# Moving three VectorE sums one step later in the queue of a blocked matrix product

## The chip, the cores and the metric

The kernel runs on one core of one Trainium2 chip. The metric is the time of one execution on the device, in microseconds (us). The profile is taken by the hardware profiler on one further execution; its span runs from the first to the last instruction.

## The reference

One layer of a diffusion transformer with a mixed sequence mixer, batch 1, 512 tokens, width 2048, float32. What matters here is the feed-forward part at its end:

```python
def conv_ffn(h, w_up, conv_w, conv_b, w_down):
    u, g = jnp.split(h @ w_up, 2, -1)
    return (u * jax.nn.silu(dwconv3(g, conv_w, conv_b))) @ w_down
...
    hx = modulate(x, sh2, sc2)
    fx = from_rows(conv_ffn(to_rows(hx), w_up[l], ffn_conv_w[l], ffn_conv_b[l], w_down[l]))
    x = layer_norm(ALPHA * x + g2 * fx, ln2_g[l], ln2_b[l])
```

`h` is 512 x 2048, `w_up` is 2048 x 11264 (u and g halves of 5632 columns each), `w_down` 5632 x 2048. `dwconv3` is a convolution of three taps along rows of 64 tokens. Ahead of it come the modulation vectors, the input projection, a gated linear recurrence in both directions, a pooling and a short convolution, and the output projection.

## The kernel before

Products of float32 are made from three products of halves: each matrix is split into a high part (a cast, on ScalarE) and a low part (what the cast left, a subtraction on VectorE). `mm3` (L109 to L113) issues high x high (L111), high x low (L112) and low x high (L113) into one PSUM place.

The changed lines belong to the stage `up_pair`, which runs 20 times, for pairs p = 2 to 21 of 128-column blocks of `w_up`, about 1330 to 2176 us into the span. Each call makes two blocks with `up_block`: first the gate's (tiles with `_g`), then u's (`_u`). A block is the product of 512 tokens with 256 columns over a depth of 2048, and is computed by a scheme of seven products over a 2 x 2 partition, as Strassen's: sums of weights and sums of activations go into seven smaller products, and four sums on VectorE give the result (L1026 to L1029, the evictions). The activations' sums (S1 to S4) are made before the stage.

A block goes through its depth in two steps (`8 // NB`, NB = 4). For each step `weights7` prepares the weights:

- the tile W, in three slots (two in the pool `ww`, one in `w3`, taken by the counter `wcount`), is loaded by two transfers of 512 KB, issued by SyncE (L989);
- three sums on VectorE fill its remaining places (L992 with 128 x 1024 elements, L993 and L994 with 128 x 512 each, each reading what the one before wrote);
- `parts` is called twice (NU = 2 of the four depth blocks each): a cast to H on ScalarE (L973), 128 x 1792 elements, and the subtraction to L on VectorE (L974). H and L have three buffers each. In what follows these are the first and the second low part of a step.

Each half step is then 7 x 2 x 3 = 42 matmuls of 128 x 256, a step 84, a pair of blocks 336. A slot of W is free again when the step's second low part is made; a buffer of H or L when TensorE has read it.

Between the blocks VectorE also makes two instructions of the gate's convolution (L936, L938) and a product with the sigmoid (L1042) for each of two column blocks, and after u's block the last products (L1047), which POOL's queue stores to `h_d`.

The order on each engine's queue is fixed when the program is traced, by a scheduler that takes what is ready in its own estimate of time, by priority; `high_priority(offset=AHEAD)` lets the weights' work go 600 places ahead of its place in the text. An engine then carries out its queue in that order, and waits where an instruction's inputs are not there. What `issue_after(x)` adds is a demand on this order alone: an instruction traced inside stands behind x in their engine's queue; it adds no signal between engines.

The stage after it, `down`, uses `parts` too, for `w_down`.

Of the kernel before, what the change touches and what calls it, by code (L numbers as in the profile page):

```python
# [1 line left out]

# [1 line left out]

# [5 lines left out]
F32 = mybir.dt.float32  # L10
# [3 lines left out]
ALU = mybir.AluOpType  # L14
# [8 lines left out]
H = 8  # L23
# [49 lines left out]
class Kernel:  # L73
# [436 lines left out]
    def pair(self, xp, gp, p, Tx, Vx):  # L510
        nc = self.nc
        qs, Qs, gs = [], [], []
        b = self.proj_x(f"q{p}", 256 * p)
        for h in range(2):
            sg = gp.tile([P, L], F32, name=f"sq_{p}_{h}", tag="sig", bufs=1)
            nc.scalar.activation(out=sg, in_=b[h], func=AF.Sigmoid)
            q = gp.tile([P, L], F32, name=f"q_{p}_{h}", tag="o", bufs=16)
            nc.vector.tensor_tensor(out=q, in0=b[h], in1=sg, op=ALU.mult)
            qs.append(q)
        if p < 2:  # L520
            T, V = Tx[p], Vx[p]
        else:
            V = xp.tile([P, NTT, 256], F32, name=f"v_{p}", tag="v", bufs=2)
            b = self.proj_x(f"v{p}", DH + 256 * p, natural=True)
            for i in range(2):
                nc.scalar.copy(out=V[:, 2 * i:2 * i + 2].rearrange("p a b -> p (a b)"), in_=b[i])
        b = self.proj_x(f"g{p}", 4 * DH + 256 * p)
        for h in range(2):
            g = gp.tile([P, L], F32, name=f"g_{p}_{h}", tag="o", bufs=16)
            nc.scalar.activation(out=g, in_=b[h], func=AF.Sigmoid)  # L530
            nc.vector.tensor_tensor(out=g, in0=b[h], in1=g, op=ALU.mult)
            gs.append(g)
        if p >= 2:
            T = [xp.tile([P, 2, L], F32, name=f"T_{2 * p + h}", tag="t", bufs=4) for h in range(2)]
        K = [xp.tile([P, 2, L], F32, name=f"K_{2 * p + h}", tag="k", bufs=2) for h in range(2)]
        for d in range(2):
            zs = [t[:, 1 - d] for t in T]
            if p >= 2:
                zs = self.proj_x(f"f{d}{p}", DH * (2 + d) + 256 * p)
            for h in range(2):  # L540
                self.gates(zs[h], T[h], K[h], d, d * H + 2 * p + h)
        for h in range(2):
            Q = gp.tile([P, 2, L], F32, name=f"Q_{p}_{h}", tag="Q", bufs=2)
            nc.vector.tensor_tensor(out=Q, in0=vw(qs[h][:, :], [[0, 2], [1, L]]), in1=T[h], op=ALU.mult)
            Qs.append(Q)
        self.steps = [self.gla(gp, 2 * p + h, qs[h], Qs[h], K[h], T[h], V[:, :, h * P:(h + 1) * P], gs[h])
                      for h in range(2)]
        self.bg_calls = 0
# [419 lines left out]
    def parts(self, ww, name, src, n):  # L968

        nc = self.nc  # L970
        H = ww.tile([P, 7 * NU * P], F32R, name=f"H_{name}", tag="H", bufs=3)
        Lw = ww.tile([P, 7 * NU * P], F32R, name=f"L_{name}", tag="L", bufs=3)
        nc.scalar.copy(out=H[:, 0:n], in_=src)  # L973
        nc.vector.tensor_tensor(out=Lw[:, 0:n], in0=src, in1=H[:, 0:n].bitcast(F32), op=ALU.subtract)  # L974
        return H, Lw

    def weights7(self, ww, name, src, c0):

        nc = self.nc
        tt = nc.vector.tensor_tensor
        with self.tc.high_priority(offset=AHEAD):
            pool, n = (ww, 2) if self.wcount % 3 < 2 else (self.w3, 1)
            self.wcount += 1
            W = pool.tile([P, NB, 7, P], F32, name=f"W_{name}", tag="W", bufs=n)
            for r0, s0 in ((c0, 2), (c0 + KT // 2, 0)):
                nc.sync.dma_start(out=vw(W[:, 0, 0, :], [[7 * P, NB], [1, 2 * P]], s0 * P),  # L989
                                  in_=src[r0 * P:(r0 + NB) * P].rearrange("(k p) c -> p k c", p=P))  # L990
            pair = lambda a, b: vw(W[:, 0, 0, :], [[7 * P, NB], [(b - a) * P, 2], [1, P]], a * P)
            tt(out=pair(4, 3), in0=pair(3, 1), in1=pair(2, 3), op=ALU.subtract)  # L992
            tt(out=W[:, :, 5], in0=W[:, :, 1], in1=W[:, :, 4], op=ALU.subtract)  # L993
            tt(out=W[:, :, 6], in0=W[:, :, 0], in1=W[:, :, 5], op=ALU.subtract)  # L994
            units = []
            for c in range(0, NB, NU):
                units += self.parts(ww, f"{name}_{c}", W[:, c:c + NU].rearrange("p a s m -> p (a s m)"), 7 * NU * P),
        return units

    def up_block(self, ww, ep, name, src):  # L1000
# [177 lines left out]
    def run(self):  # L1178
        tc, nc = self.tc, self.nc
        self.setup()  # L1180
        self.mods2 = self.persist.tile([P, 4 * KT], F32, name="mods2")
        self.o = [None] * KT
        self.h_d = [self.dram.tile([P, L], F32, name=f"h_d{f}") for f in range(NFF)]
        self.y_d = [self.dram.tile([P, 4, 512], F32, name=f"y_d{t}") for t in range(NTT)]
        self.g2_d = self.dram.tile([1, D], F32, name="g2_d")
        self.y, self.h2, self.S, self.h = {}, ({}, {}), {}, {}
        self.upc = self.wcount = 0
        with tc.tile_pool(name="wts", bufs=1, reuse_waits="tile", side="right") as self.wts:
            with tc.tile_pool(name="xp", bufs=1, reuse_waits="tile") as xp:
                self.xp = xp  # L1190
                with tc.tile_pool(name="rp", bufs=1, reuse_waits="tile") as rp:
                    self.setup_columns1(rp)
                    self.load_in(xp, rp)
                    self.setup_columns2(rp)
                    Tx, Vx = self.ramp(xp, rp)
                with tc.tile_pool(name="gp", bufs=1, reuse_waits="tile") as gp:
                    self.bg, self.bg_due, self.steps, self.bg_calls = self.ada_rest(gp), 0.0, [], 0
                    for p in (0, 2, 3):
                        self.pair(xp, gp, p, Tx, Vx)
                    self.local_setup(gp)  # L1200
                    self.conv(gp, 0)
                    self.pair(xp, gp, 1, Tx, Vx)
                    self.pool(gp, 0)
                    self.pool(gp, 1)
                    self.conv(gp, 1)
                    for st in (self.bg, *self.steps):
                        for _ in st:
                            pass
                    self.split_o()
            hctx = ExitStack()  # L1210
            hx = hctx.enter_context(tc.tile_pool(name="hx", bufs=1, reuse_waits="tile"))
            with tc.tile_pool(name="hq", bufs=1, reuse_waits="tile") as hq:
                with tc.tile_pool(name="cp", bufs=1, reuse_waits="tile") as cp:
                    st0 = self.out_half(cp, 0)
                    self.norm_mid(cp, hx, hq, 0, st0)
                    st1 = self.out_half(cp, 1)
                    for p in range(SPLIT_PAIRS):
                        self.up_half(cp, p, 0)
                    raw = self.norm_mid(cp, hx, hq, 1, st1)
                    nc.sync.dma_start(out=self.g2_d.rearrange("o (k p) -> (o p) k", p=P), in_=self.mods2[:, 3 * KT:4 * KT])  # L1220
                    for p in range(SPLIT_PAIRS):
                        self.up_half(cp, p, 1)
                        self.combine(cp, raw, (2 * p, 2 * p + 1))
        gap = self.ctx.enter_context(tc.tile_pool(name="gap", bufs=1, side="right", reuse_waits="tile"))
        gap.tile([P, 112], F32, name="gap_right")
        with tc.tile_pool(name="ww", bufs=1, reuse_waits="tile", side="right") as ww:
            with tc.tile_pool(name="ep", bufs=1, reuse_waits="tile") as ep, \
                    tc.tile_pool(name="w3", bufs=1, side="right", reuse_waits="tile") as self.w3:
                for p in range(SPLIT_PAIRS, NFF // 2):
                    self.up_pair(ww, ep, p)  # L1230
            hctx.close()
            with tc.tile_pool(name="dn", bufs=1, reuse_waits="tile") as dn:
                f0 = 0
                for i, n in enumerate(PORTIONS[:-1]):
                    self.down(ww, dn, f0, n, i == 0)
                    f0 += n
                self.finish(ww, dn, f0, PORTIONS[-1])
# [28 lines left out]
```

## Time and profile before

| | |
|---|---|
| time, median of 3 runs | 2684.64 us (2683.98 to 2686.53) |
| the profiled execution | 2687.12 us |
| its span | 2685.3 us |
| mean granted TensorE clock | 0.985 |
| TensorE busy (matmul) | 2545.6 us, 95% |
| VectorE busy | 1897.1 us, 71% |
| ScalarE busy | 928.8 us, 35% |
| GpSimd busy | 256.1 us, 10% |

Engines in the profile: PE is TensorE, PEld its weight loads, DVE VectorE, ACT ScalarE, POOL GpSimd, SP SyncE; a name with a q at its end is that engine's sequencer, which issues transfers and waits. A line of the view of waits names who waited, the source line, what ended the wait, then microseconds in total, times, and the longest. A line of a timeline gives start and length in microseconds, engine, source line, operation, tile written and tiles read, shapes, a count where several were merged, and in brackets the idle time just before it and what ended it. The granted clock is the share of full speed at which the profile says that TensorE was clocked.

### The profile page before, as it was taken

How to read it: one execution, taken by the hardware profiler on the slowest of the kernel's cores; microseconds unless marked ns; L12 is line 12 of the kernel's file. 1: busy time of each engine (PE TensorE's matmuls, PEld its weight loads, DVE VectorE, ACT ScalarE, POOL GpSimd, SP SyncE). 2: the span in 40 equal slices, each digit the busy share in tenths (PEclk: the TensorE clock that was granted, in tenths of full speed). 3: DMA queues.
4: the chain of work that ended last, by engine and by line, in shares of the span. 5: the costliest groups of instructions: out<-in, count | busy, mean ns of one | idle time of the engine just before them, and what ended most of it. 6: DMA issues, size and time to landing. Idle time of an engine off the chain costs nothing.

```text
span 2685.3 us, 40002 instructions
## 1 busy us (share of the span) xinstructions
PE 2545.6 (95%) x16332; PEld 2240.9 (83%) x16332; DVE 1897.1 (71%) x2408; ACT 928.8 (35%) x1119; POOL 256.1 (10%) x255
## 2 busy tenths in 40 slices
PE   5999999999999999999899999999999899999996
PEld 4677998888878888769899999999999888888885
DVE  5543569968698866778988889888898864433338
ACT  5221254232333324354543334433343342222111
POOL 0120102213051300001100000000000000000005
PEclk9999999999999999999999999999999999999998
DMA  8755236756646546657533333333333374333321
GB/s 266 235 181 164 87 95 224 235 167 197 204 148 209 160 128 207 209 188 243 160 111 120 109 110 118 111 107 117 116 104 125 103 247 155 127 122 131 109 94 63
DMA packets 301461, 409.85 MB, mean 153 GB/s; under 512 B 17669, under 2 KB 193117, under 8 KB 300765
## 3 DMA queue, kind: packets, MB, share of 16 engines
q1 hardware_dynamic: 297692, 395.76, 45.8%
q0 software_dynamic: 3584, 11.54, 1.1%
q8 instruction: 128, 2.10, 0.4%
q14 instruction: 57, 0.46, 0.1%
HBM read 387.30 MB, written 19.93 MB: 152 GB/s over the span
## 4 chain that ended last, share of the span: by engine, by line
PE 55%; DVE 19%; DMA 15%; issue 6%; ACT 2%; POOL 1%; SPq 1%; DVEq 0%; POOLq 0%; ACTq 0%
DMA W_g<-in_w_up_dram 7%; DMA W_u<-in_w_up_dram 6%; PE dn L113 6%; PE dn L112 6%; PE dn L111 5%; DVE L_g L974 3%; DVE L_u L974 3%; DVE W_u L992 2%; PE wo L112 2%; PE wo L113 2%; PE wo L111 1%; PE rx L111 1%; PE rc L111 1%; PE rx L113 1%; PE rc L112 1%
## 5 line engine op out<-in xcount | busy, mean ns | idle before, releaser
L974 DVE TENSOR_TENSOR L_dn<-W_dn,H_dn 128x1536 fp32r<-128x1536 f32 (+1 forms) x56 | 96.2, 1719 | 223.2 <-ACT H_dn L973 223.2
L973 ACT CAST H_u<-W_u 128x1792 fp32r<-128x1792 f32 x80 | 135.6, 1695 | 174.1 <-PE ub_g L112 171.9
L682 DVE SCALAR_TENSOR_TENSOR aacc<-a,csil,aacc 128x512 f32<-128x512 f32 x240 | 188.7, 787 | 8.3 <-DMA a<-in_w_ada_dram 3.2
L113 PE MATMUL dn<-H_dn,hl 128*128 128x512 f32 x480 | 188.6, 394 | 0.0
L112 PE MATMUL dn<-L_dn,hh 128*128 128x512 f32 x480 | 188.2, 392 | 0.0
L111 PE MATMUL dn<-H_dn,hh 128*128 128x512 f32 x480 | 185.9, 388 | 0.0
L973 ACT CAST H_dn<-W_dn 128x1536 fp32r<-128x1536 f32 (+1 forms) x56 | 81.4, 1453 | 294.9 <-PE dn L113 290.3
L974 DVE TENSOR_TENSOR L_u<-W_u,H_u 128x1792 fp32r<-128x1792 f32 x80 | 161.5, 2018 | 2.5 <-ACT H_u L973 2.5
L974 DVE TENSOR_TENSOR L_g<-W_g,H_g 128x1792 fp32r<-128x1792 f32 x80 | 161.4, 2018 | 1.0 <-ACT H_g L973 1.0
L973 ACT CAST H_g<-W_g 128x1792 fp32r<-128x1792 f32 x80 | 135.0, 1689 | 75.8 <-PE ub_g L112 55.7
L113 PE MATMUL ub_g<-h2h,L_g 128*128 128x256 f32 x480 | 137.8, 288 | 23.8 <-DVE L_g L974 23.3
L113 PE MATMUL ub_u<-h2h,L_u 128*128 128x256 f32 x480 | 136.3, 284 | 22.4 <-DVE L_u L974 22.4
L111 PE MATMUL ub_g<-h2h,H_g 128*128 128x256 f32 x480 | 134.6, 280 | 8.5 <-ACT H_g L973 8.5
L112 PE MATMUL ub_g<-h2l,H_g 128*128 128x256 f32 x480 | 134.4, 280 | 0.0
L112 PE MATMUL ub_u<-h2l,H_u 128*128 128x256 f32 x480 | 132.9, 277 | 0.0
L111 PE MATMUL ub_u<-h2h,H_u 128*128 128x256 f32 x480 | 132.8, 277 | 0.0
L105 ACT CAST wh_r<-wr_r 128x1024 fp32r<-128x1024 f32 x48 | 50.3, 1048 | 208.1 <-PE rc L113 112.4
L113 PEld LDWEIGHTS ub_g<-h2h,L_g 128*128 128x128 f32 x480 | 91.6, 191 | 29.4 <-DVE L_g L974 29.1
L113 PEld LDWEIGHTS ub_u<-h2h,L_u 128*128 128x128 f32 x480 | 90.2, 188 | 28.3 <-DVE L_u L974 28.3
L106 DVE TENSOR_TENSOR wl_wo<-wr_wo,wh_wo 128x1024 fp32r<-128x1024 f32 x64 | 78.3, 1223 | 50.0 <-ACT wh_wo L105 49.9
L112 PEld LDWEIGHTS dn<-L_dn,hh 128*128 128x128 f32 x480 | 90.1, 188 | 21.4 <-DVE L_dn L974 0.4
L992 DVE TENSOR_TENSOR W_g<-W_g 128x1024 f32<-128x1024 f32 x40 | 49.0, 1225 | 82.9 <-DMA W_g<-in_w_up_dram 82.7
(447 smaller groups left out, 8360.9 us busy)
## 6 DMA issues: line engine op xcount, KB each, us to landing
a<-in_w_ada_dram SPq DMA_DIRECT2D x256, 256.0 KB, 3.8
W_g<-in_w_up_dram SPq DMA_DIRECT2D x80, 512.0 KB, 5.4
W_u<-in_w_up_dram SPq DMA_DIRECT2D x80, 512.0 KB, 3.9
W_dn<-in_w_down_dram SPq DMA_DIRECT2D x24, 1536.0 KB, 6.7
wr_wo<-in_w_out_dram SPq DMA_DIRECT2D x64, 512.0 KB, 4.6
ada<-in_w_ada_dram SPq DMA_DIRECT2D x56, 512.0 KB, 5.0
wr_r<-in_w_in_dram SPq DMA_DIRECT2D x48, 512.0 KB, 3.7
wr_up<-in_w_up_dram SPq DMA_DIRECT2D x32, 512.0 KB, 4.5
```

Of the source, the lines that this page charges most:

```text
L105: nc.scalar.copy(out=hi, in_=raw)
L106: (lo_engine or nc.vector).tensor_tensor(out=lo, in0=raw, in1=hi.bitcast(F32), op=ALU.subtract)
L111: mm(out=out, lhsT=st[0], rhs=mv[0], start=start, stop=False)
L112: mm(out=out, lhsT=st[0], rhs=mv[1], start=False, stop=False)
L113: mm(out=out, lhsT=st[1], rhs=mv[0], start=False, stop=stop)
L682: nc.vector.scalar_tensor_tensor(out=acc, in0=raw, scalar=self.csil[:, k:k + 1], in1=acc, op0=ALU.mult, op1=ALU.add)
L973: nc.scalar.copy(out=H[:, 0:n], in_=src)
L974: nc.vector.tensor_tensor(out=Lw[:, 0:n], in0=src, in1=H[:, 0:n].bitcast(F32), op=ALU.subtract)
L992: tt(out=pair(4, 3), in0=pair(3, 1), in1=pair(2, 3), op=ALU.subtract)
```

## The change

`parts` keeps a handle on the low part that it made. `weights7` remembers the handle of its step's first low part, and traces the three sums of the next step in a context that puts them behind that instruction in VectorE's queue. The first step of the stage has no such demand. The loads, the casts and the low parts are outside the context.

```diff
-        nc.vector.tensor_tensor(out=Lw[:, 0:n], in0=src, in1=H[:, 0:n].bitcast(F32), op=ALU.subtract)
+        self.low = nc.vector.tensor_tensor(out=Lw[:, 0:n], in0=src, in1=H[:, 0:n].bitcast(F32), op=ALU.subtract)
         return H, Lw
...
             pair = lambda a, b: vw(W[:, 0, 0, :], [[7 * P, NB], [(b - a) * P, 2], [1, P]], a * P)
-            tt(out=pair(4, 3), in0=pair(3, 1), in1=pair(2, 3), op=ALU.subtract)
-            tt(out=W[:, :, 5], in0=W[:, :, 1], in1=W[:, :, 4], op=ALU.subtract)
-            tt(out=W[:, :, 6], in0=W[:, :, 0], in1=W[:, :, 5], op=ALU.subtract)
+
+            with self.tc.issue_after(self.low_first.ins) if self.low_first else nullcontext():
+                tt(out=pair(4, 3), in0=pair(3, 1), in1=pair(2, 3), op=ALU.subtract)
+                tt(out=W[:, :, 5], in0=W[:, :, 1], in1=W[:, :, 4], op=ALU.subtract)
+                tt(out=W[:, :, 6], in0=W[:, :, 0], in1=W[:, :, 5], op=ALU.subtract)
             units = []
             for c in range(0, NB, NU):
                 units += self.parts(ww, f"{name}_{c}", W[:, c:c + NU].rearrange("p a s m -> p (a s m)"), 7 * NU * P),
+                if c == 0:
+                    self.low_first = self.low
         return units
...
         self.upc = self.wcount = 0
+        self.low_first = None
```

More of the change, by code (lines that the diff above doesn't have):

```diff
@@ L1 @@
-from contextlib import ExitStack
+from contextlib import ExitStack, nullcontext
 import numpy as np
```

## The prediction

> **What bounds the kernel now.** I read the page first, then the waits of the stretch in which the changed lines run (about 1330 to 2170 us of the span), then busy time by window, then the chain of waits and the timelines of VectorE, ScalarE and TensorE there.
>
> ```profile
> DMA W_g<-in_w_up_dram 7%; DMA W_u<-in_w_up_dram 6%; PE dn L113 6%; PE dn L112 6%; PE dn L111 5%; DVE L_g L974 3%; DVE L_u L974 3%; DVE W_u L992 2%; PE wo L112 2%; PE wo L113 2%; PE wo L111 1%; PE rx L111 1%; PE rc L111 1%; PE rx L113 1%; PE rc L112 1%
> ```
>
> The page's chain of work that ended last puts 13% of the span, some 350 us, on loads of W_g and W_u. Those loads belong to one stage, the 20 calls of `up_pair`. The waits of that stage (us in total, times, longest) show who stood still:
>
> ```profile
> DVE W_g L992 <- DMA W_g<-in_w_up_dram: 82.7, 37, 4.7
> DVE W_u L992 <- DMA W_u<-in_w_up_dram: 33.6, 25, 3.1
> PE ub_g L113 <- DVE L_g L974: 23.3, 18, 2.9
> PE ub_u L113 <- DVE L_u L974: 22.4, 30, 2.8
> PE ub_g L111 <- ACT H_g L973: 8.5, 1, 8.5
> ```
>
> VectorE waits 82.7 + 33.6 = 116.3 us for weights to land, always at the first of the three sums (L992). TensorE waits 45.7 us, always for a low part (L974) from VectorE. Two windows of the stage give the size (window; busy us and instructions of PE, PEld, DVE, ACT, POOL; granted clock; DMA share; GB/s):
>
> ```profile
> 1345.00:1441.00 96.00, 95.89 (x841) 95.53 (x840) 82.73 (x82) 40.90 (x33) 2.20 (x4) 1.00 0.33 111
> 1441.00:2170.00 729.00, 685.19 (x5783) 674.35 (x5784) 614.14 (x626) 288.94 (x246) 18.61 (x34) 0.98 0.35 114
> ```
>
> In the first, TensorE runs a matmul every 96/841 = 114.2 ns with no stall. In the second it runs one every 126.1 ns: 729 - 5783 x 0.1142 = 69 us are lost. That the clock is 0.98 there is part of the loss (2% of 729 is 15 us). The mechanism is one turn of the chain of waits (start, length, what):
>
> ```profile
> 1419.34 0.37 SPq L989
> ...
> 1419.75 5.86 DMA W_u<-in_w_up_dram
> ...
> 1425.70 1.23 DVE W_u L992
> ...
> 1428.65 2.03 DVE L_g L974
> ...
> 1430.70 0.37 SPq L989
> ```
>
> A second low part frees the slot of its step's W; SyncE starts the load of the step three later; 5.86 us on it lands; VectorE, already standing at the sums of that same step, makes them and only then the next second low part, which frees the next slot. One turn is 1430.70 - 1419.34 = 11.36 us. A step is 84 matmuls, 84 x 0.1142 = 9.6 us. So the loop of load, sums and low part is longer than TensorE's work and sets the stage's pace. The next turn shows what stands behind the wait:
>
> ```profile
> 1436.63 1.23 DVE L992 TENSOR_TENSOR W_g<-W_g 128x1024 f32<-128x1024 f32 x1 [3.42 <-DMA W_g<-in_w_up_dram]
> ...
> 1439.22 2.02 DVE L974 TENSOR_TENSOR L_u<-W_u,H_u 128x1792 fp32r<-128x1792 f32 x1
> ```
> ```profile
> 1425.71 1.70 ACT L973 CAST H_u<-W_u 128x1792 fp32r<-128x1792 f32 x1 [3.06 <-PE ub_g L112]
> 1430.47 1.70 ACT L973 CAST H_u<-W_u 128x1792 fp32r<-128x1792 f32 x1 [3.06 <-PE ub_g L112]
> ```
> ```profile
> 1441.30 0.38 PE L113 MATMUL ub_u<-h2h,L_u 128*128 128x256 f32 x1 [0.41 <-DVE L_u L974]
> ```
>
> The cast that this second low part reads was done at 1430.47 + 1.70 = 1432.17. The low part started at 1439.22, 7 us later, behind 3.42 us of waiting for weights of two steps ahead and the three sums of them; TensorE came to it and stood.
>
> **The change part by part.** No instruction, byte, or place is added or removed. The stored handle and the empty context cost nothing: they exist while the program is traced. What moves is L992, L993 and L994, on VectorE alone. The two loads (L989) are outside the block and stay on SyncE's queue, and so does what frees their slot. ScalarE's and POOL's queues are passed by nothing.
>
> Now the sums of step n+2 stand between the two low parts of step n (in the rows above, sums of the next gate block between the lows of the first u step). After the change they must follow the first low part of step n+1: one step later. I take it that they stand directly behind it and before its second low part, as the present sums stand to theirs. Where that is not so is a rival.
>
> Term 1, the load. Weights for step n+3 are started as before when the second low part of step n is done. VectorE will want them behind the first low part of step n+2, about a step and a half of 9.6 us later, 14 us, less what the second low part itself ran late. Issue and load take 0.37 + 5.86 = 6.2 us. The load is covered with several us to spare, and if that cover went, the 116 us of waiting would be back. VectorE's wait of 116 us goes, and the turn of 11.36 us no longer closes inside one step.
>
> Term 2, VectorE's load without the waits. Prices from starts in a row (a start to the next start is what an instruction really takes in the queue):
>
> ```profile
> 1409.93 0.68 DVE L1042 TENSOR_TENSOR cv<-cv,cs 128x512 f32<-128x512 f32 x1
> 1410.53 0.74 DVE L936 SCALAR_TENSOR_TENSOR cv<-Z_g,col_c,cv 128x504 f32<-128x504 f32 x1
> 1411.30 0.74 DVE L938 SCALAR_TENSOR_TENSOR cv<-Z_g,col_d,cv 128x504 f32<-128x504 f32 x1
> 1411.96 2.02 DVE L974 TENSOR_TENSOR L_g<-W_g,H_g 128x1792 fp32r<-128x1792 f32 x1
> 1413.90 0.69 DVE L1042 TENSOR_TENSOR cv<-cv,cs 128x512 f32<-128x512 f32 x1
> 1414.70 1.23 DVE L992 TENSOR_TENSOR W_u<-W_u 128x1024 f32<-128x1024 f32 x1
> ...
> 1417.30 2.02 DVE L974 TENSOR_TENSOR L_g<-W_g,H_g 128x1792 fp32r<-128x1792 f32 x1
> 1419.23 0.68 DVE L1026 TENSOR_TENSOR Z_u<-ub_u,P_u 128x512 f32<-128x512 f32 x1
> ...
> 1421.81 2.02 DVE L974 TENSOR_TENSOR L_g<-W_g,H_g 128x1792 fp32r<-128x1792 f32 x1
> ```
>
> A low part is 1413.90 - 1411.96 = 1.94, the three sums 1417.30 - 1414.70 = 2.60, the four evictions of a block 1421.81 - 1419.23 = 2.58, the gate's three instructions 1411.96 - 1409.93 = 2.03, a product like L1042 0.60. A pair has four steps, two blocks, two gates, two last products: 4 x (2.60 + 2 x 1.94) + 2 x 2.58 + 2 x 2.03 + 2 x 0.60 = 36.3 us. (Check: in the long window VectorE is busy 614.14 us for 5783/336 = 17.2 pairs, 35.7 each.) TensorE needs 4 x 9.6 = 38.4 us for a pair. So TensorE becomes the bound, with VectorE at 95%. The 96-us window shows the two together without a stall, but with VectorE at 82.73/96 = 86%: the last part of the way is not shown, and is what the walk below is for.
>
> Term 3, whether so full a queue makes TensorE wait. I walk through a pair with half steps of 4.8 us, 0 being where TensorE ends the gate block. H and L have three buffers, so a cast starts when TensorE has ended the half step three before (the ScalarE rows wait for just that), and its low part can start 1.8 us later (1.70 and a signal). VectorE: gate's evictions 0 to 2.6; first low of u's second step 2.6 to 4.5, TensorE wants it at 9.6; sums of the next pair's first step and two gate instructions to 8.5; second low to 10.5, wanted at 14.4; three gate instructions to 12.5; next low to 14.5, wanted at 19.2; product and sums to 17.7; low to 19.6, wanted at 24.0; u's evictions to 22.2; low to 24.2, wanted at 28.8; sums and two products to 28.0; low to 29.9, wanted at 33.6; then the first u step's casts are the later ones: low 30.6 to 32.5, wanted at 38.4; sums to 35.1; low 35.4 to 37.4, wanted at 43.2. The least margin is 3.7 us. The sums end 0.8 to 3.3 us before the casts that read them could start anyway. So no stall is left in the steady part.
>
> The start of the stage is a term of its own:
>
> ```profile
> 1331.89 3.27 ACT L973 CAST H_g<-W_g 128x1792 fp32r<-128x1792 f32 x2 [3.90 <-issue]
> ```
> ```profile
> 1334.74 1.23 DVE L992 TENSOR_TENSOR W_g<-W_g 128x1024 f32<-128x1024 f32 x1 [2.93 <-DMA W_g<-in_w_up_dram]
> 1335.89 3.95 DVE L974 TENSOR_TENSOR L_g<-W_g,H_g 128x1792 fp32r<-128x1792 f32 x2
> ```
>
> The very first low part could start when its cast ends, 1331.89 + 3.27/2 = 1333.5, but stands behind the second step's sums until 1335.89: 2.4 us go. The 8.5 us before the stage's first matmul stay.
>
> Sum: 69 + 2.4 = 71 us at most at this pace. The walk leaves no stall, but it has no room for late sigmoids or for the first h tiles that ScalarE and VectorE split near the stage's end; I keep back 5 us, one or two stalls of the 2.9 us above with the clock lost behind them. Gain 66 us. Behind the stage the down projection keeps its order, so I carry the gain to the end in full. Bounds of the unknown part: no loss at all in the window at TensorE's own pace, which the two rows
>
> ```profile
> 1442.10 0.28 PE L113 MATMUL ub_u<-h2h,L_u 128*128 128x256 f32 x1
> ...
> 1447.20 0.28 PE L113 MATMUL ub_u<-h2h,L_u 128*128 128x256 f32 x1
> ```
>
> give as 5.10/45 = 113.3 ns: 729 - 5783 x 0.1133 + 2.4 = 76 us; and below, half of the loss staying, 35 us.
>
> The profiled execution took 2687.12 us, 2.5 us above the median of the runs, so from 2684.64: 2684.6 - 66 = 2618.6.
>
> **A rule beside the rows.** In the Trainium skill, "TensorE: Matmul & The Clock Gate", Part 1, an idle window of about 3.4 us halves TensorE's clock, and the clock returns after as long a busy one. This trace agrees so far: 0.98 in the window with stalls, 1.00 in the one without. By that rule stalls that only grow shorter would give back those 15 us even if they stayed as many. The same page, "Back-to-back issue gap", gives N/2.4 + 2.5 ns when warm, an estimated 109.2 ns for 256 columns, by which the gain could reach 729 - 5783 x 0.1092 = 97 us; the rows of 113.3 ns, measured where nothing waits, decide against it.
>
> **The rivals.** *The sums fall behind both low parts.* If VectorE's order becomes first low, second low, sums, then the cast of the next step can start only behind the sums, and the next low part 1.8 us behind them. VectorE idles that long once a step unless evictions lie there: 36.3 + 4 x 1.8 = 43.5 us a pair against 729/17.2 = 42.4 now, 20 x 1.1 = 22 us slower, 2707. It decides from (42.4 - 36.3)/4 = 1.5 us of idling a step. For it: a queue at 95% can well have both low parts ready at once (two lie together, x2, in the row at 1335.89). Against: in steady state casts of one step come 1430.47 - 1425.71 = 4.8 us apart, so the second low is not ready when the first ends, and 10 us of evictions and products a pair would fill most of 7.2. *VectorE becomes the bound in part*: sums late behind evictions, then cast, then low; half the loss stays, 2650. For it: 36.3 of 38.4. Against: the margins of 3.7 us. *Nothing moves that counts*: the order asked for is already the order, or the load's wait only changes place; 2684.6. Against it stand the 3.42 us in front of the later low part and sums that run a step earlier than the new rule allows. A measurement of this kernel can tell about 0.2%, 5 us, from no change.
>
> **How the numbers follow.** Main case 0.74 (2608 to 2635), VectorE bound in part 0.13 (2635 to 2675), nothing 0.04, behind both lows and slower 0.09. Faster 0.87, same 0.04, slower 0.09. The low end is the bound of 76 us, 2608; the high end 2656 takes in the half loss and leaves out about 0.17.
>
> **What would show it.** Right: VectorE's wait at L992 for W falls from 116 us to under 15, TensorE's for L974 from 45.7 to under 10, the clock is near 1.00 from 1345 on, one matmul each 114 to 115 ns there, loads of W gone from the chain, VectorE's busy time unchanged, the down stage unchanged in length. Wrong: ScalarE's casts wait for L994 some 1.8 us a step, VectorE's low parts for casts, TensorE's waits stay; or the sums still stand in front of the first low part of the step before theirs.

## The result, and the profile after

The changed kernel takes 2612.1 us (median of 4 runs, 2611.17 to 2613.28), against 2684.41 us for the kernel before beside it: a ratio of 0.9729, 95% interval 0.9712 to 0.9746, 72.3 us less. The forecast was 2618.6 us. The profiled execution took 2612.17 us.

The page's chain of work that ended last, by engine, has turned over. Before, DMA held 15% of it and TensorE 55%; after, 3% and 81%:

```profile
PE 55%; DVE 19%; DMA 15%; issue 6%; ACT 2%; POOL 1%; SPq 1%; DVEq 0%; POOLq 0%; ACTq 0%
```
```profile
PE 81%; DVE 8%; issue 4%; DMA 3%; ACT 2%; POOL 1%; SPq 0%; DVEq 0%; ACTq 0%; POOLq 0%
```

In the waits of the stage (who waited, for whom, us in total, times, longest) VectorE no longer waits for any load of W, and TensorE's 45.7 us of waiting for low parts are gone. What is left to TensorE is the one wait at the start, the same 8.5 us as before. VectorE now waits for casts:

```profile
DVE L_u L974 <- ACT H_u L973: 36.1, 19, 2.2
DVE Z_g L1030 <- PE ub_g L113: 6.4, 16, 0.5
DVE L_g L974 <- ACT H_g L973: 3.6, 2, 1.8
...
PE ub_g L111 <- ACT H_g L973: 8.5, 1, 8.5
```

The windows (busy us and instructions of PE, PEld, DVE, ACT, POOL, then clock, DMA share, GB/s) that answer to the two shown before:

```profile
1345.00:1441.00 96.00, 96.00 (x850) 96.00 (x849) 88.62 (x89) 44.39 (x37) 2.19 (x4) 1.00 0.38 124
1441.00:2095.00 654.00, 654.00 (x5773) 654.00 (x5772) 606.21 (x621) 295.44 (x244) 18.54 (x34) 1.00 0.38 125
```

5773 matmuls took 654 us where 5783 had taken 729. TensorE is busy throughout, at the full granted clock. The order is seen in VectorE's timeline (start, length, line, tile; lines after L991 have moved down by two to four: L994 to L996 are the three sums, L1051 a last product):

```profile
1419.13 2.02 DVE L974 TENSOR_TENSOR L_g<-W_g,H_g 128x1792 fp32r<-128x1792 f32 x1
1421.06 1.22 DVE L994 TENSOR_TENSOR W_u<-W_u 128x1024 f32<-128x1024 f32 x1
1422.20 0.68 DVE L1051 TENSOR_TENSOR cv<-Z_u,cv 128x512 f32<-128x512 f32 x1
1422.80 0.68 DVE L995 TENSOR_TENSOR W_u<-W_u 128x512 f32<-128x512 f32 x1
...
1424.00 2.02 DVE L974 TENSOR_TENSOR L_g<-W_g,H_g 128x1792 fp32r<-128x1792 f32 x1
1425.94 0.68 DVE L996 TENSOR_TENSOR W_u<-W_u 128x512 f32<-128x512 f32 x1
1428.51 2.02 DVE L974 TENSOR_TENSOR L_u<-W_u,H_u 128x1792 fp32r<-128x1792 f32 x1 [1.89 <-ACT H_u L973]
```

The sums of u's first step now stand between the two low parts of the gate's second step, one step ahead of their own low parts; their weights landed 9 us before (1412.21 us), so L994 starts where L974 ends.

### The profile page after: what moved, and what is told of

Its sections match the earlier page's. It is cut to its first block, busy times and chain, and to the rows that moved or that the text cites. A ratio compares the mean times of both kernels' runs of the same rounds, so it can differ in the third digit from the quotient of the medians.

```text
span 2610.4 us, 40021 instructions
## 1 busy us (share of the span) xinstructions
PE 2516.4 (96%) x16332; PEld 2221.3 (85%) x16332; DVE 1893.3 (73%) x2408; ACT 937.8 (36%) x1119; POOL 255.9 (10%) x255
## 4 chain that ended last, share of the span: by engine, by line
PE 81%; DVE 8%; issue 4%; DMA 3%; ACT 2%; POOL 1%; SPq 0%; DVEq 0%; ACTq 0%; POOLq 0%
PE dn L112 6%; PE dn L111 6%; PE dn L113 6%; PE ub_g L113 5%; PE ub_g L111 5%; PE ub_g L112 5%; PE ub_u L113 5%; PE ub_u L112 5%; PE ub_u L111 5%; PE wo L112 2%; PE wo L113 2%; PE wo L111 2%; PE rx L111 2%; DVE aacc L682 1%; PE rx L113 1%
## 5 line engine op out<-in xcount | busy, mean ns | idle before, releaser
L974 DVE TENSOR_TENSOR L_dn<-W_dn,H_dn 128x1536 fp32r<-128x1536 f32 (+1 forms) x56 | 96.2, 1718 | 224.5 <-ACT H_dn L973 224.4
L974 DVE TENSOR_TENSOR L_u<-W_u,H_u 128x1792 fp32r<-128x1792 f32 x80 | 161.7, 2021 | 38.0 <-ACT H_u L973 36.1
L974 DVE TENSOR_TENSOR L_g<-W_g,H_g 128x1792 fp32r<-128x1792 f32 x80 | 161.2, 2017 | 3.6 <-ACT H_g L973 3.6
L111 PEld LDWEIGHTS dn<-H_dn,hh 128*128 128x128 f32 x480 | 90.1, 188 | 20.9
L113 PEld LDWEIGHTS dn<-H_dn,hl 128*128 128x128 f32 x480 | 90.1, 188 | 19.9
L112 PE MATMUL wo<-wl_wo,oh 128*128 128x512 f32 x256 | 103.0, 402 | 4.1 <-DVE wl_wo L106 4.0
L112 PEld LDWEIGHTS dn<-L_dn,hh 128*128 128x128 f32 x480 | 90.2, 188 | 18.6 <-DVE L_dn L974 0.4
```

The source lines that it names most:

```text
L111: mm(out=out, lhsT=st[0], rhs=mv[0], start=start, stop=False)
L112: mm(out=out, lhsT=st[0], rhs=mv[1], start=False, stop=False)
L113: mm(out=out, lhsT=st[1], rhs=mv[0], start=False, stop=stop)
L974: self.low = nc.vector.tensor_tensor(out=Lw[:, 0:n], in0=src, in1=H[:, 0:n].bitcast(F32), op=ALU.subtract)
```

## The experiments

Two readings had to be told apart. **The loop:** before the change, slot, load, sums and second low part close a loop inside one step, longer than TensorE's step, and the change opens it. **The place:** the low parts simply gain by not standing behind sums that nobody needs yet, or VectorE's work as such is the bound. They ran in groups on one chip each, with the kernel before beside them (2685.74 to 2688.31 us); times are medians, ratios are to that kernel.

**Two slots for W.** The changed order is kept, and the loop is closed again by taking a slot away.

```diff
-            pool, n = (ww, 2) if self.wcount % 3 < 2 else (self.w3, 1)
+            pool, n = ww, 2
```

> The changed kernel with two slots for W in place of three (the tile in w3 is not used). VectorE's queue is as in the changed kernel but for one pair of neighbours. Theory (the loop of slot, load, sums and second low part set the pace): with two slots the load of step n+2 starts behind the second low part of step n, and the sums of step n+2 stand between the two low parts of step n+1, so the loop closes inside one step again as it did before the change: 0.37 + 5.9 + 2.6 + 2.0 us and signals, about 11.3 us a step. Time 2670 to 2700 us, VectorE waiting for W at L994 for 100 us or more, TensorE for L974 for 40 us or more. Rival (the gain comes from the sums' new place itself, in that a low part no longer stands behind sums that nobody needs yet): the place is kept, so 2612 to 2625 us.

Measured: 2685.44 us, ratio 0.9988 (0.9977 to 0.9999). In the time of the execution the whole gain is gone, to within 3 us. The waits of the stage are back:

```profile
DVE W_u L994 <- DMA W_u<-in_w_up_dram: 52.8, 37, 3.6
...
DVE W_g L994 <- DMA W_g<-in_w_up_dram: 23.9, 23, 3.7
...
PE ub_u L113 <- DVE L_u L974: 21.7, 30, 3.2
PE ub_g L113 <- DVE L_g L974: 18.9, 15, 3.2
```

The sums stand where the change puts them and VectorE's queue differs in one pair of neighbours. So their place alone is worth nothing; the distance from the freeing of a slot to the use of what is loaded into it is what counts. From the first to the last matmul of the stage this kernel took 835.3 us, 10.44 us a step, the kernel before 842.3, 10.53 a step: 7 of the 78.5 us that the change gains there (below) are left, and a first matmul that comes 6.8 us later than in the kernel before hides them. (VectorE's wait, 76.7 us, fell short of the 100 expected: it waits 41.5 us for casts as well.)

**Half a step.** This is the smallest move that opens the loop.

```diff
-                if c == 0:
-                    self.low_first = self.low
+        self.low_first, self.low_next = self.low_next, self.low
         return units
```

> The sums moved by half a step in place of a whole one: behind the second low part of the step two before. Theory: the load of step n+2 starts behind the second low part of step n-1, the sums stand behind that of step n, 9.5 us later; issue and load take 6.2 us, so the load is covered by some 3 us and nearly all of the gain is there: 2608 to 2622 us, VectorE's wait for W under 20 us. Rival (the whole step is needed, since a load sometimes takes up to 7.3 us and low parts run late): part of the waits stays, 2630 to 2660 us.

Measured: 2617.92 us, ratio 0.9764 (0.9716 to 0.9813; one of its four runs took 2644.93 us, on which more below). In its profile VectorE waits for W once, 3.0 us, at the stage's start, and TensorE waits 2.3 us there for the first low part. The loop's reading holds; a whole step is not needed.

**Behind both low parts.** This is the order of the prediction's rival for "slower".

```diff
-                if c == 0:
-                    self.low_first = self.low
+                self.low_first = self.low
```

> The changed kernel with the sums behind the second low part of the preceding step, not the first. Theory: the load stays covered, so no wait for W; the cast of the next step starts only behind the sums. VectorE's queue shows evictions between the sums and the next low part in two of the four steps of a pair, two products of 0.6 us in the third and nothing in the fourth, so some 1.8 + 0.6 us of idling a pair: 36.3 + 2.4 = 38.7 us against TensorE's 38.1, 2612 to 2630 us. The prediction's rival had priced this order at 43.5 us a pair with all of the idling open, 2707 us. If the place of the sums alone matters (rival), two low parts in a row make TensorE's waits vanish and the time is at or below 2612 us.

Measured: 2614.74 us, ratio 0.9733 (0.9717 to 0.9749): as the changed kernel. VectorE's waits for casts in the stage are larger than there, and TensorE waits for none of it:

```profile
DVE L_u L974 <- ACT H_u L973: 47.6, 40, 2.2
DVE L_g L974 <- ACT H_g L973: 15.4, 21, 1.8
...
PE ub_g L111 <- ACT H_g L973: 8.5, 1, 8.5
```

63 us in 20 pairs is 3.2 us a pair, not 7.2: the scheduler laid evictions between sums and low parts, as the rival's "against" had it.

**Each load twice, in both kernels.** The same edit to the changed kernel and to the kernel before.

```diff
+                for _ in range(2):
-                nc.sync.dma_start(...)
+                    nc.sync.dma_start(...)
```

> The changed kernel with each load of W in the blocks made twice, one behind the other into the same place. Theory: the changed order leaves the load about a step and a half, some 13 us; a load of 10 to 12 us and its issue still fit, or nearly: 2612 to 2630 us, VectorE's wait for W under 40 us in all. Rival (the loads were short of bandwidth and the gain is one of fewer collisions): twice the bytes cost more than 80 us, 2690 us or above.

Measured: 2620.99 us, ratio 0.9776 (0.9728 to 0.9824; again one run of four apart, 2647.95). Twice the bytes (233 GB/s in place of 125 in the window from 1441 us) cost the changed kernel 9 us against its 2612.1, and those lie ahead of the stage's first matmul, which comes at 1346.3 us in place of 1337.2: TensorE's wait there grew from 8.5 to 15.4 us. In the stage VectorE waits for W once, 6.9 us, at its start, and TensorE for nothing else.

> The kernel before with each load of W in the blocks made twice, one behind the other into the same place, as in the changed kernel with doubled loads, and no demand on the order. The scheduler, which reckons with the longer load, now puts the sums of step n+2 behind the second low part of step n by itself, half a step later than in the kernel before. Theory: what the kernel before lacks is that half step and not bandwidth; the load of about 10.7 us closes its loop over two steps (10.7 + 2.6 + 2 x 1.9 and evictions, 17 to 20 us against 19.0), so the time is 2615 to 2660 us, faster than the kernel before with twice its bytes. Rival (the load's length itself is the cost, wherever the sums stand): some 5 us more in each of 80 steps, 2900 us or more.

Measured: 2654.49 us, ratio 0.9890 (0.9865 to 0.9914): with twice its bytes, and no demand on the order, the kernel before becomes 1.1% faster. The sums stand half a step later in VectorE's queue than in the kernel before, behind the second low part and not between the two. It fits this that the scheduler reckons with a longer load here, and with too short a one in the kernel before; its estimates are in no record, so this is not shown. VectorE waits 71.4 + 20.6 us for W here, for the load now barely fits, but TensorE waits only 3.9 us for low parts; of the 39 us by which it lies above the changed kernel run beside it (2615.71 us), 27 are a longer pace of the matmuls (below), which 5937 of the stage's 6719 have here.

**One sum twice, in both kernels.** VectorE's work raised by 2.4 us a pair.

```diff
+                tt(out=W[:, :, 6], in0=W[:, :, 0], in1=W[:, :, 5], op=ALU.subtract)
                 tt(out=W[:, :, 6], in0=W[:, :, 0], in1=W[:, :, 5], op=ALU.subtract)
```

> The kernel before with the last of the three sums of a step made twice (0.6 us of VectorE more a step, 2.4 us a pair). In the queue the extra instruction lies between the first sum and the second low part in two of four steps, and one gate instruction has moved out from there in a third. Theory (the loop of slot, load, sums and second low part sets the pace): what counts is what lies between the first sum and the second low part, about 0.55 us a pair more, and VectorE's waiting for loads takes up the rest: 2690 to 2710 us. Rival (VectorE's work is the bound of the kernel before): 80 x 0.61 = 49 us more, 2730 us or above.

Measured: 2697.9 us, ratio 1.0035 (1.0021 to 1.0049), 10 us more and not 49. VectorE's wait for W took up most of the work, falling from 116.3 to 75.4 us, as the work grew by 48:

```profile
DVE W_g L992 <- DMA W_g<-in_w_up_dram: 58.2, 25, 4.2
DVE W_u L992 <- DMA W_u<-in_w_up_dram: 17.2, 16, 3.3
```

So VectorE's amount of work did not bound the kernel before.

> The changed kernel with the last of the three sums of a step made twice. VectorE is busy 35.2 us a pair in the changed kernel, so 37.6 here, against TensorE's 38.1; the queue now has both low parts of a step in a row ahead of the sums. Theory (TensorE is the bound, VectorE has some 2.9 us a pair to spare): 2612 to 2640 us. Rival (VectorE at 95% is already what sets the changed kernel's pace): 49 us more, 2660 us.

Measured: 2675.09 us, ratio 0.9958 (0.9943 to 0.9972). My expectation failed and the rival's number came nearer. But the profile shows no VectorE that is merely full:

```profile
DVE L_u L974 <- ACT H_u L973: 62.9, 40, 2.2
...
PE ub_g L113 <- DVE L_g L974: 19.1, 36, 0.9
...
DVE L_g L974 <- ACT H_g L973: 14.2, 21, 1.8
...
PE ub_u L113 <- DVE L_u L974: 9.2, 26, 0.7
```

VectorE idles 77 us for casts while TensorE waits for low parts. The scheduler had put both low parts in a row with the four sums behind them, and sums, cast and low parts became a chain that VectorE cannot leave: 821.1/20 = 41.1 us a pair, near the sum of its work (35.3 + 2.4) and its waits (3.9), 41.6. This is the prediction's rival at work, by this reading: it decides once the work in that order leaves no room for the waits, which the run before it in that order (2614.74 us) just had.

Because order and work had changed together, two more kernels load VectorE in another place, with the weights' work left in the changed order: an eviction made three and five times.

```diff
-        tt(out=Z[:, 5], in0=place[7], in1=Z[:, 4], op=ALU.add)
+        for _ in range(3):
+            tt(out=Z[:, 5], in0=place[7], in1=Z[:, 4], op=ALU.add)
```

> The changed kernel with the second eviction of a block (L1032 here, 128 x 256, 0.46 us from start to start) made three times in place of once: 4 x 0.46 = 1.84 us of VectorE more a pair, with the low parts and sums in the changed order. Theory (TensorE is the bound of the changed kernel, and VectorE waits 36.1 + 6.4 + 3.6 + 1.9 = 48 us in its 20 pairs, 2.4 us each, to spare): within 6 us of the changed kernel on the same kind of chip, 2612 to 2621 us. Rival (VectorE is already the bound): 20 x 1.84 = 37 us more, 2650 us.

> The same with the second eviction made five times: 8 x 0.46 = 3.7 us of VectorE more a pair, now beyond the 2.4 us to spare. Theory: 20 x (3.7 - 2.4) = 26 us more than the changed kernel, 2630 to 2650 us, with TensorE waiting for low parts again. Rival (VectorE is already the bound): 74 us more, 2685 us.

Measured: three times, 2631.5 us (ratio 0.9803, 0.9737 to 0.9869), five times, 2636.1 us (0.9833, 0.9791 to 0.9875). The medians mislead: the runs of each fall in two groups, 2613.79 and 2616.44 against 2646.56 and 2647.40 for the first, 2626.03 and 2627.25 against 2644.95 and 2645.45 for the second. In both profiles the view of waits has no wait of TensorE for a low part in the stage. With five, VectorE is 98% busy and TensorE is busy throughout:

```profile
1441.00:2095.00 654.00, 654.00 (x5665) 653.86 (x5665) 640.04 (x745) 283.24 (x238) 18.46 (x34) 1.00 0.37 121
```

So TensorE is the bound of the changed kernel, as the theory has it. The expected 26 us for the second kernel rested on a wrong price: VectorE's busy time grew from 35.3 to 640.04/(5665/336) = 38.0 us a pair, so 2.7 us a pair were added and not 3.7, about what was to spare. That is more than the doubled sum had added (2.4), without its waits: here sums still stand between the low parts. What sets these runs apart is the pace of the matmuls:

```profile
1499.82 0.28 PE L112 MATMUL ub_u<-h2l,H_u 128*128 128x256 f32 x1
...
1505.12 0.28 PE L112 MATMUL ub_g<-h2l,H_g 128*128 128x256 f32 x1
```
```profile
1499.80 0.28 PE L112 MATMUL ub_g<-S1l,H_g 128*128 128x256 f32 x1
...
1504.90 0.28 PE L112 MATMUL ub_g<-S2l,H_g 128*128 128x256 f32 x1
```

Above is the kernel with three evictions (the execution of 2647.40 us), below the changed kernel: 45 matmuls lie between the rows, 5.30/45 = 117.8 ns each against 5.10/45 = 113.3, both without a wait and at a granted clock of 1.00. In the first, 6694 of the stage's 6719 distances have the longer pace: 6694 x 4.5 ns = 30 us, which is the distance of the two groups.

The profiled execution with five evictions, 2626.03 us, has both paces. It keeps the shorter one up to 1782 us; there a matmul comes about 0.1 us late, right behind the low part that it reads (made at 1782.41 us), and 2809 distances at the longer pace follow, to the stage's end:

```profile
1782.33 0.28 PE L112 MATMUL ub_u<-h2l,H_u 128*128 128x256 f32 x1
1782.46 0.39 PE L113 MATMUL ub_u<-h2h,L_u 128*128 128x256 f32 x1
1782.69 0.28 PE L111 MATMUL ub_u<-h2h,H_u 128*128 128x256 f32 x1
```

2809 x 4.5 ns = 12.6 us, so this execution too is the changed kernel's time, 2613.4 us, and a longer pace.

**The changed kernel again, twice.** It was run beside the second four, and then with five rounds on a further chip.

> The changed kernel once more, beside the others on one chip: 2610 to 2616 us.

> The changed kernel a third time, to see how often its TensorE takes the longer pace. In the trace of the kernel with two extra evictions all but 25 matmuls of the stage follow at 118 ns, without a wait, and that execution took 2647 us; in the traces of the changed kernel all follow at 113 to 114 ns, 2612 and 2615 us. If the pace is taken at the start of the stage and held where nothing interrupts TensorE, the times fall in two groups with little between, 2611 to 2618 us and 2640 to 2650 us (6700 x 4.7 ns = 31 us apart), the second in about one of five. If the longer pace belongs to the extra evictions, all are 2611 to 2618 us.

Measured: 2615.71 us (ratio 0.9768, 0.9696 to 0.9841; one run of four at 2646.2), and 2613.23 us, 2610.52 to 2616.32, ratio 0.9721 (0.9708 to 0.9734). One of 13 runs of the changed kernel lies by its time in the slower group, so that group does not belong to the extra evictions alone. That the pace is always taken at the stage's start is refuted by the turn at 1782 us above. How often the longer one comes, five runs without it could not tell, nor whether extra evictions make it more frequent (4 of their 8 runs took 2644 us or more). No variant beats the changed kernel.

## Why the prediction was right, step by step

**The order.** Taken as sums behind the first low part of the preceding step and before its second: so it is, with one difference. The third sum often slips behind the second low part (L996 at 1425.94 above), so the cast of u's first step starts at 1426.78 instead of before it is wanted, and VectorE waits about 1.9 us, 19 times. The walk had put 0.7 us there. It cost nothing: TensorE waited for no low part, and the least margin of the walk was 3.7 us.

**Term 1, the load.** Covered, as forecast: 116.3 us of waiting went to none. The load with twice its bytes shows the margin of several us to be real, the two slots show what happens when the cover goes. The turn of 11.36 us that the prediction showed was one of the longest: from one second low part to the next, 79 turns of the kernel before took 10.46 us on average, and 14 of them over 11. The sum does not use it.

**Term 2, VectorE's load.** 36.3 us a pair forecast; 606.21/(5773/336) = 35.3 measured, against 654/(5773/336) = 38.1 of TensorE. TensorE became the bound.

**Term 3, the walk.** No stall was left in the steady part. Distances of over 300 ns between matmuls of the stage fell from 58 to 3.

**The start.** The first low part now starts as soon as its cast is done, 1335.51 + 1.70 to 1337.22. The first low-part matmul comes 2.1 us behind the stage's first matmul in place of 4.4: the 2.4 us were there.

**The sum** was 69 + 2.4 - 5 = 66 us; from the first to the last matmul the stage shrank from 842.3 to 763.8, 78.5 us. Two terms were mis-sized. The 5 us held back were not needed. And the pace of 114.2 ns, taken from a window nearly without stalls, was itself not clean: mainly, 81 of its matmuls followed at 118 ns, from 1431 us on. Over the 6719 distances between the stage's matmuls, those over 300 ns gave back 55.4 us, those of 150 to 300 ns (half clock, and what follows a stall) 18.6, those near 118 ns 4.1: 78.1 of the 78.5. The upper bound in the prediction, 76 us, had used 113.3 ns, the right pace. That 72.3 and not 78.5 us show in the medians has two plain parts: in these two profiled executions the work ahead of the stage, which the change leaves alone, ended 3.6 us later in the second (first matmul at 1333.6 and 1337.2), and the profiled execution of before lay 2.7 us above its median. Behind the stage both took 509.4 us. So it is in part luck that 66 lies as near to the measured 72.3 as it does: the stage gave 12 us more than forecast.

**The clock.** 0.98 became 1.00, and with no wait left, the rule of "TensorE: Matmul & The Clock Gate", Part 1, in the Trainium skill had nothing to bite on. The trace of before agreed with that rule less than the prediction says: its longest stall in the stage from 1345 us on, 2.9 us, is shorter than the window of about 3.4 us, and the clock fell all the same (last section). The 109.2 ns, an estimate from the formula that the same page of the Trainium skill gives for the isolated gap of a matmul ("Back-to-back issue gap"), were not reached; the clean pace is 113.3.

**The rivals.** "Behind both low parts" was priced at 2707 us and takes 2614.74: 7.2 us of idling a pair was an upper end, 3.2 came. The mechanism exists, as the doubled sum in that order shows. "VectorE the bound in part" did not come; "nothing moves that counts" fell with the first row of waits.

## What to carry to other kernels

Where an engine that works through its queue in order waits for a load, ask what stands behind the wait, and whether that is what frees the slot for the next load: then load and work add up in a loop, and the loop's mean length against the bound engine's step tells the gain: 10.53 us a step (842.3/80) against 9.55 (763.8/80) here. Moving the consumer half a step later opened the loop without another buffer; and taking a buffer away is a clean test of it. An order that was fixed by an estimate deserves a second look: making the load dearer in the program moved the work to a better place.

## What the runs showed of the hardware

Two paces of matmul without any wait: 113.3 and 117.8 ns for the same instruction, at the same granted clock. A pace holds until something interrupts TensorE, if only by 0.1 us: in the kernel before it turned to the longer one behind a delay of about 0.1 us and back at the next stall:

```profile
1430.73 0.39 PE L113 MATMUL ub_g<-h2h,L_g 128*128 128x256 f32 x1
1430.95 0.28 PE L111 MATMUL ub_g<-h2h,H_g 128*128 128x256 f32 x1
...
1436.25 0.28 PE L111 MATMUL ub_u<-h2h,H_u 128*128 128x256 f32 x1
```

(45 matmuls in 5.30 us.) Not every stall turns it back: behind the one that ended at 1581.2 us in the kernel before, 82 distances at the longer pace follow. A kernel whose TensorE is never late keeps the pace it has, for better or worse; what sets it stays open.

The half clock does not follow every long stall, and the length of a stall alone does not decide. Idle times before three low-part matmuls of the kernel before, and windows behind each (the clock is the third number from the right):

```profile
1496.24 0.38 PE L113 MATMUL ub_u<-h2h,L_u 128*128 128x256 f32 x1 [2.83 <-DVE L_u L974]
...
1834.28 0.38 PE L113 MATMUL ub_u<-h2h,L_u 128*128 128x256 f32 x1 [2.56 <-DVE L_u L974]
...
2106.08 0.38 PE L113 MATMUL ub_g<-h2h,L_g 128*128 128x256 f32 x1 [2.38 <-DVE L_g L974]
```
```profile
1497.70:1500.70 3.00, 3.00 (x16) 3.00 (x16) 2.96 (x4) 1.78 (x2) 0.00 (x0) 0.50 0.98 333
...
2106.50:2109.50 3.00, 3.00 (x29) 3.00 (x28) 2.06 (x2) 0.37 (x1) 0.00 (x0) 1.00 0.78 235
1834.50:1840.00 5.50, 5.50 (x36) 5.50 (x36) 5.31 (x7) 2.57 (x4) 0.00 (x0) 0.69 0.58 191
```

2.83 and 2.56 us of idling were followed by half clock, 2.38 us was not. But in the kernel with two slots 3.23 us was not either, and in the kernel before with one sum twice 2.22 us was:

```profile
2109.22 0.38 PE L113 MATMUL ub_g<-h2h,L_g 128*128 128x256 f32 x1 [3.23 <-DVE L_g L974]
```
```profile
2109.30:2112.30 3.00, 3.00 (x26) 3.00 (x27) 1.12 (x2) 2.37 (x2) 0.29 (x1) 1.00 0.58 183
```
```profile
1775.99 0.45 PE L113 MATMUL ub_g<-h2h,L_g 128*128 128x256 f32 x1 [2.22 <-DVE L_g L974]
```
```profile
1776.30:1779.30 3.00, 3.00 (x16) 3.00 (x16) 2.86 (x3) 0.00 (x0) 0.35 (x1) 0.50 0.64 180
```

In the clock records of every trace, all changes of the granted clock lie on a grid of 3.413 us. In the stage, from 15 us after its start, the clock fell at the end of each window of that grid in which TensorE had idled for 1.91 us or more (13 windows, in four of the kernels), and of none in which it had idled for 1.76 us or less. The 3.23 us lay across two windows, 1.73 and 1.51 us; the 2.22 us lay in one. The Trainium skill's page named above speaks, in Part 1, of an idle window of about 3.4 us; here 1.91 us of one were enough.
